# dt columns from the two f32r parts of h on the full array; one diagonal burst per scan group, two bursts per latent convolution tile

## The chip, the core and the metric

The kernel runs on one core of one Trainium2 chip. The metric is the device time of one execution in microseconds (us). Three runs of the kernel before the change took 1979.71, 1980.26 and 1985.91 us; the median is 1980.26 us. The profiled execution has a span of 1980.4 us from its first to its last instruction.

A core has these engines, named as the profile names them: PE (TensorE, matrix multiplication; its weight loads are listed apart as PEld and overlap the matmuls), DVE (VectorE), ACT (ScalarE), POOL (GpSimd) and SP (SyncE, from whose queue all DMAs of this kernel are issued). Each engine works through its own list of instructions in order, and waits where an operand is not there.

## The reference, cut to what matters

One layer of a diffusion backbone, for 256 context tokens and 2048 latent tokens, 1024 channels wide. All data are float32.

```python
h = rms_norm(x, g_pre) * (1 + scale) + shift
u = h @ w_in                       # 1024 x 5664
z, xbc, dt_raw, ga, gb, gsil = split(u)   # 1024, 1536, 32, 1024, 1024, 1024 columns
y_ssd, h_fin = ssd_branch(z, xbc, dt_raw, ...)     # two-way scan, 16 heads of 64, chunks of 128
y_conf = conformer_branch(ga, gb, ...) * silu(gsil)  # 31-tap convolution, layer norm
out = concat([y_ssd, y_conf]) @ w_out
return x + gate * rms_norm(out, g_post), h_fin
```

Three pieces of it are touched: `dt_raw`, the 32 columns of the input projection that give the step sizes of the scan; the part of the scan inside a chunk, `y_diag = (C B^T * decay) x`, one 128x128 matrix per head and chunk; and the 31-tap convolution of the latent tokens along the rows of a 32x64 grid.

## The kernel before, in words

**Stages.** The 2304 tokens are 18 chunks of 128, done in two halves of nine; a half is three blocks of 384 tokens. In each half `hprep` makes h for a block, transposed, channels on the partitions, in two f32r parts: `hh` (h rounded) and `hl` (the rest). Then tiles of 128 columns of `w_in` (also in two parts, `wh` and `wl`) are multiplied: `mm_cm` (L334) runs over eight slices k of the channels, with three matmuls of 128x384 each (L338 to L340), into the psum tiles `xp` (x, B, C), `gb`/`ga` (gate) and `sp` (z and gsil). `xbc_unit` and `conv5` follow each xp tile with a five-tap convolution on DVE. While the gb, ga and sp tiles run, the scan (`pass_a`, chunk by chunk) is woven in; in the first half with it the context convolution on DVE, in the second half the latent convolution (`lat_conv`, eight tiles of 128 channels). At the end comes the output projection (`op`, L1038).

**hprep (L237).** Per block: `pr` spreads the norm over the partitions (L271); for each of the eight slices k, DVE multiplies the slice `ht` by it (L285), ACT applies scale and shift (L288), and `split(k)` (L274) does the rest: the dt matmul on PE (L277), the cast to `hh` on DVE (L278), and the subtraction that gives `hl` on POOL, for every fourth slice on DVE (L279). The dt matmul is in plain f32 with 32 columns of weights; slice k goes to columns `32*(k%4)` of the array, so that `pd` holds four partial sums that L304 adds after a transposition.

**The scan (L606).** `pass_a(i)` is a generator of about ten steps per chunk, and the next chunk starts six steps after the one before. Each chunk has two groups g of eight heads, and each group two quarters hq of four heads with two directions. `load_lb` (L617) loads 256 KB of row data, spread to all partitions, into the tiles `lb` (four buffers per direction); `mask`, `decay` and `mix` make the 128x128 matrices of four heads out of them; `diag(g, hq)` (L671) then multiplies four of them on PE into `py`, each with 64 columns of weights (head j of a pair in columns 64j). `off` gives `po` (L684), `state` the three matmuls of `pst` (L690 to L692).

**The latent convolution (L559).** `expand(u)` (L574) copies taps into one of two buffers `kbuf`, eight small copies, four on DVE and four on ACT; then eight matmuls with 64 columns of weights go into `cp` (L592). There are four such rounds per tile, with a step between.

**What sets the order.** The generators are interleaved by hand (`interleave`, `merge`, `xbc_phase`), but the lists of the engines are set when the kernel is built: the program is scheduled with a timeline simulation (`schedule_with_timeline_sim=True`, L1182), which moves instructions by when it reckons that they can start. So the order of the source is a wish, and the lists are what stands. [...]

Of the kernel before, what the change touches and what calls it, by code (L numbers as in the profile page):

```python
# [8 lines left out]
F32 = mybir.dt.float32  # L9
F32R = mybir.dt.float32r  # L10
# [3 lines left out]
MUL, ADD, SUB, MAX, MIN = ALU.mult, ALU.add, ALU.subtract, ALU.max, ALU.min  # L14
# [31 lines left out]
def merge(a, na, b, nb):  # L46
    """The steps of two generators as one list, each spread evenly over it."""
    steps, x, y = [], 0, 0
    for _ in range(na + nb):
        if y * na >= x * nb and x < na or y >= nb:  # L50
            steps.append(a)
            x += 1
        else:
            steps.append(b)
            y += 1
    return steps
# [8 lines left out]
def backbone_kernel(ctx, tc, xa, xt_in, cols, rows, wconv, conf_b, gp_row, bg_row, state0, w_mod, w_dt, w_in, w_out,  # L65
# [8 lines left out]
    def bank(tag, name):  # L74
        return psp.tile([P, 512], F32, tag=tag, name=name, bufs=3 if tag == "mm" else 5)
# [75 lines left out]

    # ---------------------------------------------------------------- input projection, scan, convolutions
    ph_h = ExitStack()
# [26 lines left out]
    V.tensor_scalar(cfb2, cv[:, C_CONFB:C_CONFB + 8], 2.0, None, MUL)  # L180
    wdt = pa.tile([P, KT, 32], F32, name="wdt")
    DT = pa.tile([P, HTILES, 32], F32, name="DT")
# [4 lines left out]

    # ---- modulation
    sc = pa.tile([P, 2, 8], F32, name="sc")
# [12 lines left out]
    def modulation(h):  # L202
        """Shift and scale of one half of the channels, as columns."""
        mp = bank("mm", f"mp{h}")
        for k in range(KT):
            if h == 1 and k in (3, 4):
                wm = pa.tile([P, 2, 512], F32, tag=("xT", "el")[k - 3], name=f"wm{h}_{k}", bufs=1)
            elif h == 1 and k > 4:
                wm = cp.tile([P, 2, 512], F32, tag="x4", name=f"wm{h}_{k}", bufs=3)
            else:  # L210
                if k % 3 == 0:
                    b, tag = ((1, "a"), (1, "b"), (2, "a"), (2, "b"))[3 * h + k // 3]
                    wms, n = hps[b].tile([P, 3, 2, 512], F32, tag=tag, name=f"wm{h}_{k}"), 0
                wm = wms[:, n]
                n += 1
            DMA.dma_start(wm, w_mod[k * P:(k + 1) * P, 0:2 * D].rearrange("p (s c) -> p s c", s=2)[:, :, h * 512:(h + 1) * 512])
            for s in range(4):
                T.matmul(mp[32 * s:32 * s + 2, 0:256], sc[:, :, k], wm[:, s // 2, s % 2 * 256:s % 2 * 256 + 256],
                         start=(k == 0), stop=(k == KT - 1))
            yield  # L220
        mc = bank("ss", f"mc{h}")
        mr = slab(f"mr{h}")
        for s in range(4):
            (V.tensor_copy if s % 2 else S.copy)(mr[0:2, s * 256:(s + 1) * 256], mp[32 * s:32 * s + 2, 0:256])
            for q in range(2):
                c = 2 * s + q
                T.transpose(mc[:, 2 * c:2 * c + 2], mr[0:2, c * P:(c + 1) * P], ident[0:2, 0:2])
        m = mc[:, 0:16].rearrange("p (s k a) -> p s a k", s=2, k=4)
        ks = slice(4 * h, 4 * h + 4)
        bc4 = lambda c: cv[:, c + 4 * h:c + 4 * h + 4].unsqueeze(1).to_broadcast([P, 2, 4])  # L230
        V.scalar_tensor_tensor(S1[:, :, ks], m[:, 1], 1.0, bc4(C_BSC), ADD, ADD)
        V.tensor_tensor(S1[:, :, ks], S1[:, :, ks], bc4(C_GPRE), MUL)
        V.tensor_tensor(SH[:, :, ks], m[:, 0], bc4(C_BSH), ADD)
        yield

    # ---- normalised, modulated, transposed input of one block in two f32r parts; its dt columns
    def hprep(b, out):  # L237
# [34 lines left out]
        pd = bank("ss", f"pd{b}")  # L272

        def split(k):  # L274
            t = ts.pop(k)
            q = k % 4
            T.matmul(pd[q * 32:(q + 1) * 32, :BN], wdt[:, k, :], t, start=(k < 4), stop=(k >= 4))  # L277
            V.tensor_copy(hh[:, k, :], t)  # L278
            (V if k % 4 == 3 else G).tensor_tensor(hl[:, k, :], t, hh[:, k, :].bitcast(F32), SUB)  # L279

        for k in range(KT):
            if b > 0:
                load_t(k)
            t = ts[k]
            V.tensor_tensor(t, t, pr[:, :BN], MUL)  # L285
            parts = ((0, 256, 1), (256, BN, 0)) if b == 0 else ((0, BN, 0),)
            for c0, c1, a in parts:
                S.activation(t[:, c0:c1], t[:, c0:c1], AF.Identity, bias=SH[:, a, k:k + 1], scale=S1[:, a, k:k + 1])  # L288
            if k > 0 and not (b == 0 and k == 4):
                split(k - 1)  # L290
            if b == 0 and k == 3:
                split(k)
            yield
        split(KT - 1)
        yield
        d4 = ev(f"d4_{b}")
# [3 lines left out]
        for t in range(BLK):  # L300
            T.transpose(pt[:, t * P:(t + 1) * P], d4[:, t * P:(t + 1) * P], ident)
        yield
        t0 = (b % BLK) * BLK
        V.tensor_reduce(DT[:, t0:t0 + BLK, :], pt[:, :BN].rearrange("p (t q h) -> p t h q", t=BLK, q=4),  # L304
                        mybir.AxisListType.X, ADD)
        yield

    # ---- one tile of input-projection columns, split in two f32r parts
    def load_w(c0):
# [32 lines left out]

    # ---- dt: softplus, its logarithm, and the decays of every chunk
    def dt_post(half):
# [64 lines left out]

    # ---- x, B, C columns and their five-tap convolution along the tokens  # L410
    def xbc_unit(half, ct, hb, tails):
# [36 lines left out]
    def xbc_phase(half, first, hb, prep, tails, dtp):  # L448
        """The first tiles go block by block, while the next block is being prepared."""
        def tail_step():  # L450
# [57 lines left out]

    # ---- gate of the modulation times g_post, as two rows in DRAM
    def gate_rows():  # L510
# [23 lines left out]

    # ---- Conformer convolution of the context tokens, along the sequence
    def ctx_conv(j):
# [20 lines left out]

    # ---- Conformer convolution of the latent tokens, along the rows of the grid
    def lat_conv(j, lp, kbuf):  # L559
# [24 lines left out]
        yield  # L584
        expand(0)
        yield
        for u in range(4):
            kt = kbuf[u % 2]
            ps = bank("ss", f"cp{j}_{u}")
            for q in range(4):  # L590
                for h in range(2):
                    T.matmul(ps[h * 64:(h + 1) * 64, q * P:(q + 1) * P], x[:, h * 16 + u * 4 + q, :], kt[:, h * 4 + q, :],  # L592
                             start=True, stop=True)
            if u < 3:
                expand(u + 1)
            yield
            V.scalar_tensor_tensor(vt[:, ::-1, u * 16:(u + 1) * 16].rearrange("p r c -> p c r"),
                                   ps.rearrange("p (c r) -> p c r", r=32), 0.5,
                                   cbb[:, u * 16:(u + 1) * 16].unsqueeze(2).to_broadcast([P, 16, 32]), MUL, ADD)
# [4 lines left out]

    # ---- scan of one chunk: inside the chunk both ways, across chunks forward
    def pass_a(i):  # L606
# [63 lines left out]

        def diag(g, hq):  # L671
            if hq == 0:
                py[g] = bank("ss", f"py{i}{g}")
            for t in range(4):
                h = hq * 4 + t
                j, q = h % 2, h // 2
                T.matmul(py[g][j * HD:(j + 1) * HD, q * P:(q + 1) * P], xt[g][:, h * HD:(h + 1) * HD],
                         E[g, hq, 0][:, t, :], start=True, stop=True)

# [75 lines left out]
        yield  # L755
        diag(0, 0)
        off(0)
# [6 lines left out]
        yield  # L764
        diag(0, 1)
        state(0, 1)
# [4 lines left out]
        yield  # L771
        diag(1, 0)
        off(1)
        state(1, 0)
        weigh(1, 1)
        keep(0)
        close(0)
        mix(1, 1)
        yield
        diag(1, 1)  # L780
        state(1, 1)
# [10 lines left out]
    def scan(tiles):  # L792
        """Chunks in turn, each starting six steps after the one before it."""
        gens = [pass_a(i) for i in tiles]
        live, t = [], 0
        while gens or live:
            if gens and t % 6 == 0:
                live.append(gens.pop(0))
            for g in list(live):
                if next(g, 0) == 0:  # L800
                    live.remove(g)
            t += 1
            yield

    # ---- order of the work
    def interleave(blocks, side, n):
# [29 lines left out]
    run(modulation(0))  # L836
    DMA.dma_start(wdt.rearrange("p k n -> p (k n)"), w_dt)
    for _ in range(4):
# [57 lines left out]

    # ---------------------------------------------------------------- output projection
    ph_1 = ExitStack()
# [288 lines left out]
```

## Time and profile before

| | before |
|---|---|
| runs (us) | 1979.71, 1980.26, 1985.91 |
| median (us) | 1980.26 |
| span of the profiled execution (us) | 1980.4 |
| mean granted TensorE clock | 0.976 |
| busy, share of the span: PE, PEld | 96%, 85% |
| busy, share of the span: DVE, ACT, POOL | 64%, 44%, 42% |
| DMA: bytes moved, mean rate | 306.03 MB, 155 GB/s |

How to read the rows. A row of a timeline gives the start in us from the start of the span, the duration in us, the engine, the line, the operation, the tile written and those read, weights and result sizes, and how many records were merged into the row; what follows in brackets is the idle time of the engine before it and what ended it. Matmuls are pipelined and their ends are modelled, so the time that a matmul takes is read from one start to the next. A plain f32 matmul leaves two records (x2), an f32r matmul one; both are labelled f32. A row of windows gives, for a stretch of time, how long each engine was busy, the granted clock of PE, the DMA share and the rate.

### The profile page before, as it was taken

The page shows a single profiled execution, that of the slowest core. Times are in us where ns is not written, and L with a number is a line of the kernel's source. Part 1 is how long each engine was busy: PE and PEld are TensorE (multiplying, and loading weights), DVE is VectorE, ACT ScalarE, POOL GpSimd, SP SyncE. Part 2 cuts the span into 40 slices and gives each one's busy share as a digit, 9 for nine tenths or more (in the row PEclk, how much of TensorE's full clock was granted, in tenths as well). Part 3 has the DMA queues.
Part 4 walks back from the last instruction along what each step waited for, and adds up shares of the span by engine and source line. Part 5 has one row for each costly group of instructions (what it writes and reads, how often), then busy time and mean ns, then how long its engine had stood idle before and what let it go on. Part 6 is the DMA issues. An engine that isn't in the chain of part 4 may idle for free.

```text
span 1980.4 us, 29842 instructions
## 1 busy us (share of the span) xinstructions
PE 1892.3 (96%) x10796; PEld 1693.0 (85%) x10796; DVE 1273.9 (64%) x1776; ACT 869.1 (44%) x1973; POOL 830.0 (42%) x760
## 2 busy tenths in 40 slices
PE   7999999979998999998999999999999999999998
PEld 4699988979887897898999999989997878778776
DVE  2587768797765425878556665565438766776753
ACT  3447333443444523455356665664424333333332
POOL 2435243444443524544246455453226443454421
PEclk8999999989999999999999999999999999999999
DMA  8325453434344633233556667664947555555542
GB/s 294 118 93 158 138 145 123 121 107 133 118 144 135 207 134 106 96 112 112 153 148 190 189 194 212 177 192 148 282 155 198 160 163 155 176 169 156 161 131 78
DMA packets 285105, 306.03 MB, mean 155 GB/s; under 512 B 84630, under 2 KB 207382, under 8 KB 284956
## 3 DMA queue, kind: packets, MB, share of 16 engines
q1 hardware_dynamic: 284956, 304.12, 50.4%
q8 instruction: 85, 1.39, 0.3%
q14 instruction: 64, 0.52, 0.1%
HBM read 221.38 MB, written 82.67 MB: 154 GB/s over the span
## 4 chain that ended last, share of the span: by engine, by line
PE 54%; DVE 12%; DMA 6%; issue 4%; ACT 4%; POOL 2%; SPq 1%; DVEq 0%; POOLq 0%; ACTq 0%
PE op L1038 15%; PE sp L338 4%; PE sp L340 4%; PE sp L339 4%; DVE cg L546 4%; PE ga L338 2%; PE ga L340 2%; PE ga L339 2%; PE gb L338 2%; DVE cva L440 2%; PE gb L339 2%; PE gb L340 2%; DMA lb<-lt 2%; ACT lb L641 2%; PE cp L592 1%
## 5 line engine op out<-in xcount | busy, mean ns | idle before, releaser
L318 POOL TENSOR_TENSOR wl<-wr,wh 128x512 fp32r<-128x512 f32 x176 | 265.8, 1526 | 259.7 <-ACT wh L317 237.8
L338 PE MATMUL sp<-hh,wh 128*128 128x384 f32 x768 | 264.6, 344 | 11.9 <-DVE sth L506 11.8
L339 PE MATMUL sp<-hl,wh 128*128 128x384 f32 x768 | 260.9, 340 | 0.0
L340 PE MATMUL sp<-hh,wl 128*128 128x384 f32 x768 | 260.9, 340 | 0.0
L641 ACT ACTIVATE lb<-lb,WB 128x128 f32<-128x128 f32 x576 | 180.2, 390 | 93.9 <-POOL lb L633 89.3
L338 PE MATMUL xp<-hh,wh 128*128 128x384 f32 x576 | 199.6, 347 | 12.1 <-ACT raw L428 9.8
L340 PE MATMUL xp<-hh,wl 128*128 128x384 f32 x576 | 198.1, 344 | 0.3 <-POOL wl L318 0.3
L339 PE MATMUL xp<-hl,wh 128*128 128x384 f32 x576 | 198.4, 345 | 0.0
L633 POOL TENSOR_SCALAR_AFFINE_SELECT lb<-lb 128x512 f32<-128x512 f32 x144 | 118.2, 831 | 180.7 <-DMA lb<-lt 105.7
L440 DVE SCALAR_TENSOR_TENSOR cva<-raw,cwh,cva 128x1026 f32<-128x1026 f32 (+1 forms) x96 | 157.7, 1650 | 27.7 <-ACT cva L434 25.9
L317 ACT CAST wh<-wr 128x512 fp32r<-128x512 f32 x176 | 102.5, 616 | 136.3 <-DMA wr<-in_w_in 74.4
L338 PEld LDWEIGHTS sp<-hh,wh 128*128 128x128 f32 x768 | 145.7, 190 | 18.6 <-DVE sth L506 13.8
L546 DVE SCALAR_TENSOR_TENSOR cg<-cg,cv 128x256 f32<-128x256 f32 x240 | 156.6, 669 | 4.0
L339 PEld LDWEIGHTS sp<-hl,wh 128*128 128x128 f32 x768 | 145.9, 190 | 2.8 <-issue 1.6
L340 PEld LDWEIGHTS sp<-hh,wl 128*128 128x128 f32 x768 | 145.6, 190 | 2.1 <-issue 2.0
L1016 ACT ACTIVATE th<-ct,lnq 128x128 f32<-128x128 f32 x144 | 65.9, 457 | 184.9 <-PE ct L1012 84.2
L506 DVE SCALAR_TENSOR_TENSOR sth<-sth,sp 128x384 f32<-128x384 f32 x96 | 52.4, 550 | 136.1 <-ACT sth L505 130.6
L338 PE MATMUL ga<-hh,wh 128*128 128x384 f32 x384 | 132.8, 346 | 0.0
L340 PE MATMUL ga<-hh,wl 128*128 128x384 f32 x384 | 130.5, 340 | 2.2 <-POOL wl L318 2.2
L338 PE MATMUL gb<-hh,wh 128*128 128x384 f32 x384 | 131.9, 344 | 0.3 <-DVE gth L495 0.3
L339 PE MATMUL ga<-hl,wh 128*128 128x384 f32 x384 | 130.6, 340 | 0.0
L338 PEld LDWEIGHTS xp<-hh,wh 128*128 128x128 f32 x576 | 110.3, 192 | 23.5 <-ACT raw L428 11.3
(228 smaller groups left out, 4505.0 us busy)
## 6 DMA issues: line engine op xcount, KB each, us to landing
wr<-in_w_in SPq DMA_DIRECT2D x176, 256.0 KB, 3.2
lb<-lt SPq DMA_DIRECT2D x144, 256.0 KB, 3.9
ht<-in_xt SPq DMA_DIRECT2D x48, 192.0 KB, 3.3
xT<-xb SPq DMA_DIRECT2D x18, 512.0 KB, 5.4
gl<-gth SPq DMA_DIRECT2D x48, 192.0 KB, 2.5
yp<-yg SPq DMA_DIRECT2D x36, 256.0 KB, 3.9
st<-sb SPq DMA_DIRECT2D x36, 256.0 KB, 3.7
zs<-sth SPq DMA_DIRECT2D x48, 192.0 KB, 2.2
```

The costliest lines, as they stand in the source:

```text
L317: S.copy(wh[:, ks, :], wr)
L318: G.tensor_tensor(wl[:, ks, :], wr, wh[:, ks, :].bitcast(F32), SUB)
L338: T.matmul(ps[:, :BN], wh[:, k, :], hh[:, k, :], start=(k == 0), stop=False)
L339: T.matmul(ps[:, :BN], wh[:, k, :], hl[:, k, :], start=False, stop=False)
L340: T.matmul(ps[:, :BN], wl[:, k, :], hh[:, k, :], start=False, stop=(k == KT - 1))
L440: V.scalar_tensor_tensor(a[:, :n], raw[:, t:t + n], cwh[:, ct * 5 + t:ct * 5 + t + 1], a[:, :n], MUL, ADD)
L506: V.scalar_tensor_tensor(th, th, 1.0, ps[:, :BN], ADD, MUL)
L546: V.scalar_tensor_tensor(acc, g[:, t:t + 256], cv[:, w0 + t:w0 + t + 1], acc, MUL, ADD)
L633: G.affine_select(E[g, hq, d], E[g, hq, d], pattern=[[0, 4], [sg, P]], compare_op=ALU.is_ge, fill=NEG, base=0, channel_multiplier=-sg)
L641: S.activation(lb[:, h, :], lb[:, h, :], AF.Exp, bias=WB[:, i, c + h:c + h + 1])
L1016: S.activation(th[:, c, :], pc, AF.Tanh, bias=lnq[:, 1, k:k + 1], scale=lnq[:, 0, k:k + 1])
L1038: T.matmul(pso[n], lhs[:, k % 8, :], w[:, n * 512:(n + 1) * 512], start=(k == 0 and m == 0), stop=(k == 15 and m == 2))
```

## The change

Three things are rewritten, and the lists of all engines are scheduled anew.

**dt columns.** `split` no longer issues the dt matmul. A new `dt_cols(k)` issues two f32r matmuls per slice, with `hh` and with `hl`, over the full 128 columns of the array. The weights `wdt` are an f32r tile in which slice k has 64 columns: 32 of the rounded weights, 32 of the rest; the matmul takes 128 columns from there on, so the upper 64 rows of `pd` hold products that nobody reads. It is issued three steps later than the slice is prepared, and the last three after a further step. L304 now adds two partial sums, not four. The weights are loaded to `wdr`, and split once by two small DVE operations.

**Diagonal matmuls.** `diag(g)` issues the eight matmuls of a group in one go, at the step where the second quarter was before. `mix(1, 1)` moves ahead of `keep(0)` and `close(0)`.

**Latent convolution.** `expand(0)` and `expand(1)` go first, then the matmuls of rounds 0 and 1 together, `expand(2)` and `expand(3)`, a step, then rounds 2 and 3 together. A tile has five steps where it had seven.

Beside that the scratch memory for dynamic DMAs is set to 1024 bytes, which makes room in SBUF, and comments are gone.

```diff
-    wdt = pa.tile([P, KT, 32], F32, name="wdt")
+    wdr = pa.tile([P, KT, 32], F32, name="wdr")
+    wdt = pa.tile([P, KT * 64 + 64], F32R, name="wdt")
+    G.memset(wdt[:, KT * 64:].bitcast(F32), 0.0)
...
+        def dt_cols(k):
+
+            w = wdt[:, k * 64:k * 64 + P]
+            T.matmul(pd[:, :BN], w, hh[:, k, :], start=(k == 0), stop=False)
+            T.matmul(pd[:, :BN], w, hl[:, k, :], start=False, stop=(k == KT - 1))
+
         def split(k):
             t = ts.pop(k)
-            q = k % 4
-            T.matmul(pd[q * 32:(q + 1) * 32, :BN], wdt[:, k, :], t, start=(k < 4), stop=(k >= 4))
             V.tensor_copy(hh[:, k, :], t)
...
+            if k > 2:
+                dt_cols(k - 3)
             yield
         split(KT - 1)
+        yield
+        for k in range(KT - 3, KT):
+            dt_cols(k)
         yield
...
-        V.tensor_reduce(DT[:, t0:t0 + BLK, :], pt[:, :BN].rearrange("p (t q h) -> p t h q", t=BLK, q=4),
+        V.tensor_reduce(DT[:, t0:t0 + BLK, :], pt[:, :BN].rearrange("p (t q h) -> p t h q", t=BLK, q=4)[:, :, :, 0:2],
...
         expand(0)
-        yield
+        expand(1)
+        yield
+        ps2 = {}
         for u in range(4):
-            kt = kbuf[u % 2]
-            ps = bank("ss", f"cp{j}_{u}")
-            for q in range(4):
-                for h in range(2):
-                    T.matmul(ps[h * 64:(h + 1) * 64, q * P:(q + 1) * P], x[:, h * 16 + u * 4 + q, :], kt[:, h * 4 + q, :],
-                             start=True, stop=True)
-            if u < 3:
-                expand(u + 1)
-            yield
+            if u % 2 == 0:
+                for v in (u, u + 1):
+                    ps2[v] = bank("ss", f"cp{j}_{v}")
+                    for q in range(4):
+                        for h in range(2):
+                            T.matmul(ps2[v][h * 64:(h + 1) * 64, q * P:(q + 1) * P], x[:, h * 16 + v * 4 + q, :],
+                                     kbuf[v % 2][:, h * 4 + q, :], start=True, stop=True)
+                if u == 0:
+                    expand(2)
+                    expand(3)
+                yield
+            ps = ps2.pop(u)
...
-        def diag(g, hq):
-            if hq == 0:
-                py[g] = bank("ss", f"py{i}{g}")
-            for t in range(4):
-                h = hq * 4 + t
+        def diag(g):
+            py[g] = bank("ss", f"py{i}{g}")
+            for h in range(8):
                 j, q = h % 2, h // 2
                 T.matmul(py[g][j * HD:(j + 1) * HD, q * P:(q + 1) * P], xt[g][:, h * HD:(h + 1) * HD],
-                         E[g, hq, 0][:, t, :], start=True, stop=True)
+                         E[g, h // 4, 0][:, h % 4, :], start=True, stop=True)
...
-        diag(0, 0)
         off(0)
...
-        diag(0, 1)
+        diag(0)
...
-        diag(1, 0)
         off(1)
         state(1, 0)
         weigh(1, 1)
+        mix(1, 1)
         keep(0)
         close(0)
-        mix(1, 1)
-        yield
-        diag(1, 1)
+        yield
+        diag(1)
...
-    DMA.dma_start(wdt.rearrange("p k n -> p (k n)"), w_dt)
+    DMA.dma_start(wdr.rearrange("p k n -> p (k n)"), w_dt)
+    wd4 = wdt[:, 0:KT * 64].rearrange("p (k q n) -> p k q n", q=2, n=32)
+    V.tensor_copy(wd4[:, :, 0, :], wdr)
+    V.tensor_tensor(wd4[:, :, 1, :], wdr, wd4[:, :, 0, :].bitcast(F32), SUB)
```

Three places in the list of PE show how the instructions stand. The first is the start of block 1 in the first half; `xp_2_0` is the projection of the third column tile for block 0, `xp_0_1` and its fellows are those for block 1, `pd` is the dt tile of block 1. Before, from the last of the `pr` matmuls of block 1 on:

```order
L271 MATMUL pr_582<-ident,xr_577 128x128
L340 MATMUL xp_2_0_552<-hh_179,wl_85_392 128x384
L338 MATMUL xp_2_0_552<-hh_179,wh_85_393 128x384
L339 MATMUL xp_2_0_552<-hl_180,wh_85_393 128x384
...
L277 MATMUL pd_586<-ht_0_587,wdt 32x384
L338 MATMUL xp_2_0_552<-hh_179,wh_85_393 128x384
L339 MATMUL xp_2_0_552<-hl_180,wh_85_393 128x384
L277 MATMUL pd_586<-ht_1_597,wdt 32x384
L277 MATMUL pd_586<-ht_2_607,wdt 32x384
```

And now:

```order
L273 MATMUL pr_594<-ident,xr_589 128x128
L279 MATMUL pd_598<-hh_568,wdt 128x384
L349 MATMUL xp_0_1_690<-hh_568,wh_87_375 128x384
L349 MATMUL xp_1_1_769<-hh_568,wh_86_385 128x384
L349 MATMUL xp_2_1_830<-hh_568,wh_85_395 128x384
L280 MATMUL pd_598<-hl_569,wdt 128x384
L279 MATMUL pd_598<-hh_568,wdt 128x384
```

Before, 22 projection matmuls of block 0 stood between `pr` and the first that needs `hh` of block 1; now there is none, since those of `xp_2_0` moved up into block 0. At `pr` of block 2, 21 projection matmuls stand there now.

The second place is the start of block 4 in the second half, where `xp_2_0` is again a projection for the block before. Before:

```order
L277 MATMUL pd_7144<-ht_4_7202,wdt 32x384
L339 MATMUL xp_2_0_7267<-hl_6891,wh_41_7095 128x384
L277 MATMUL pd_7144<-ht_5_7215,wdt 32x384
L340 MATMUL xp_2_0_7267<-hh_6890,wl_41_7094 128x384
L277 MATMUL pd_7144<-ht_6_7225,wdt 32x384
L338 MATMUL xp_2_0_7267<-hh_6890,wh_41_7095 128x384
```

And now:

```order
L279 MATMUL pd_7180<-hh_7150,wdt 128x384
L349 MATMUL xp_2_0_7305<-hh_6918,wh_41_7131 128x384
L350 MATMUL xp_2_0_7305<-hl_6919,wh_41_7131 128x384
L351 MATMUL xp_2_0_7305<-hh_6918,wl_41_7130 128x384
...
L280 MATMUL pd_7180<-hl_7151,wdt 128x384
L279 MATMUL pd_7180<-hh_7150,wdt 128x384
```

The matmuls with 32 columns are gone; two of full width per slice, one with `hh` and one with `hl`, took their place, and the first needs `hh` where only `ht` was needed before. Between `pr` of this block and the first `pd` now stand 46 projection matmuls of the block before.

The third place is a group of the scan in the second half. Before, a burst of four `py` matmuls stood ahead of `po`, and the second, later, ahead of `pst`:

```order
L340 MATMUL ga_1_1_8938<-hh_7114,wl_28_8555 128x384
L677 MATMUL py_8945<-lb_8682,xt_8815 64x128 x4
L684 MATMUL po_8950<-bc_8679,Sf_173 128x128 x4
L690 MATMUL pst_8955<-xwh_8870,bth_8809 128x512
L691 MATMUL pst_8955<-xwl_8871,bth_8809 128x512
```

Now `po` follows a projection directly, and the eight `py` matmuls stand together where the second four stood:

```order
L351 MATMUL gb_1_2_9068<-hh_7351,wl_29_8597 128x384
L691 MATMUL py_9081<-lb_8734,xt_8867 64x128 x4
L691 MATMUL py_9081<-lb_8830,xt_8867 64x128 x4
L704 MATMUL pst_9090<-xwh_9007,bth_8861 128x512
L705 MATMUL pst_9090<-xwl_9008,bth_8861 128x512
```

Over the whole list the bursts of `py` go from 72 to 36, those of `cp` from 31 to 17 (the four rounds of the last tile stood in two bursts already), and the 44 bursts with `pd` are gone.

More of the change, by code (lines that the diff above doesn't have):

```diff
@@ L1177 @@
     arrays = {f"in_{k}": np.ascontiguousarray(v) for k, v in arrays.items()}
-    nc = _bacc.Bacc("TRN2", target_bir_lowering=False, num_devices=1)
+    nc = _bacc.Bacc("TRN2", target_bir_lowering=False, num_devices=1, dynamic_dma_scratch_size=1024)
     args = [nc.dram_tensor(k, v.shape, mybir.dt.from_np(v.dtype), kind="ExternalInput").ap() for k, v in arrays.items()]
```

## The prediction

> **What bounds the kernel now.** I read the engines' shares, then the stretches with the granted clock, then the timeline of PE around the instructions that change.
>
> ```profile
> PE 1892.3 (96%) x10796; PEld 1693.0 (85%) x10796; DVE 1273.9 (64%) x1776; ACT 869.1 (44%) x1973; POOL 830.0 (42%) x760
> 60.00:100.00 40.00, 39.52 (x191) 27.58 (x190) 26.13 (x42) 15.10 (x29) 15.62 (x15) 1.00 0.30 100
> 260.00:500.00 240.00, 222.86 (x1310) 208.55 (x1309) 191.82 (x300) 97.94 (x254) 98.32 (x99) 0.96 0.41 120
> 745.00:810.00 65.00, 65.00 (x303) 45.09 (x303) 38.05 (x63) 26.11 (x51) 29.53 (x30) 1.00 0.35 108
> 1000.00:1250.00 250.00, 250.00 (x1725) 227.61 (x1723) 150.57 (x239) 161.26 (x424) 133.23 (x127) 1.00 0.64 187
> ```
>
> The reader sees that PE is the bound. In 745 to 810, where half of the dt matmuls stand, and in 1000 to 1250, with the second scan and the latent convolution, it never idles: a microsecond saved on PE there is one saved at the end, unless another engine becomes late. Only the first scan (260 to 500) leaves PE 17 us idle at 0.96 of the clock, beside a DVE busy for 80%.
>
> **The price of a dt matmul.** Durations overlap, so I take starts.
>
> ```profile
> L277 PE MATMUL pd<-ht,wdt 128*32 128x384 f32 x96 | 39.9, 527 | 4.6 <-ACT ht L288 4.6
> 752.96 0.34 PE L339 MATMUL sp<-hl,wh 128*128 128x384 f32 x1
> 753.23 0.83 PE L277 MATMUL pd<-ht,wdt 128*32 128x384 f32 x2
> 753.99 0.44 PE L340 MATMUL sp<-hh,wl 128*128 128x384 f32 x1
> 754.36 0.83 PE L277 MATMUL pd<-ht,wdt 128*32 128x384 f32 x2
> 755.12 0.45 PE L338 MATMUL sp<-hh,wh 128*128 128x384 f32 x1
> 755.40 0.33 PE L339 MATMUL sp<-hl,wh 128*128 128x384 f32 x1
> 755.58 0.34 PE L340 MATMUL sp<-hh,wl 128*128 128x384 f32 x1
> 69.51 0.84 PE L277 MATMUL pd<-ht,wdt 128*32 128x384 f32 x4
> ```
>
> A projection matmul follows the next by 0.175 us (755.40 to 755.58). From 752.96 to 755.40 pass 2.44 us with three of them (0.525) and two dt matmuls: 0.96 each. A new one is a pair of the projection's own form (f32r, 128x384, full width), 0.35. There are 48 (96 records, two for each). Two neighbours run together and cost as one (the x4 row): in the second half 24 stand in 23 bursts, in blocks 1 and 2 there are 16 in 13.
>
> Second half: 23 x 0.96 less 24 x 0.35 is **13.7 us**, all in a stretch where PE never idles. What could hold it back is the preparation of the next block, since the first `pd` now waits for `hh`, not `ht`. The first half shows how long that takes:
>
> ```profile
> 60.43 0.83 PE L271 MATMUL pr<-ident,xr 128*128 128x128 f32 x6
> 61.30 3.81 DVE L285 TENSOR_TENSOR ht<-ht,pr 128x384 f32<-128x384 f32 x8
> 65.09 3.42 DVE L278 CAST hh<-ht 128x384 fp32r<-128x384 f32 x5
> 66.17 4.47 POOL L279 TENSOR_TENSOR hl<-ht,hh 128x384 fp32r<-128x384 f32 x4
> 78.62 0.83 PE L271 MATMUL pr<-ident,xr 128*128 128x128 f32 x6
> ```
>
> DVE does its eight products first, so the first `hh` is there 5.4 us after `pr` (65.09 and one cast of 0.7), the first `hl` some 1.5 us later (66.17 and a quarter of 4.47), and then one per 1.1. In the second half 46 projection matmuls, 8.0 us, stand between `pr` and the first `pd`: that covers it, and I cost the wait at nothing. Without that cover it is the first half's case.
>
> There, blocks 1 and 2 save 13 x 0.96 less 16 x 0.35, 6.9 us, and block 0 at most 8 x 0.61, 4.9. But the list has nothing left between `pr` of block 1 and its `hh`: 5.4 less 0.6 for `pr` itself, 4.8 us idle. At block 2 the 21 matmuls (3.7 us) leave 1.1. And the clock falls:
>
> ```profile
> 337.56 0.79 PE L691 MATMUL pst<-xwl,bth 128*128 128x512 f32 x1 [3.47 <-DVE xwl L668]
> 340.46 0.34 PE L338 MATMUL ga<-hh,wh 128*128 128x384 f32 x1
> ```
>
> After 3.47 us of idling matmuls take twice as long for 2.9 us, a loss of 1.4. So 11.8 less 4.8, 1.1 and 1.4 leaves 4.5; since PE also waited in block 0 for `ht` (the 4.6 of the group row), part of block 0's saving only lengthens a wait: I take **3 us**, bounds 0 and 11.
>
> **The price of a burst.** A burst of 64-column matmuls has edges:
>
> ```profile
> 1000.82 0.34 PE L340 MATMUL ga<-hh,wl 128*128 128x384 f32 x1
> 1001.09 1.09 PE L592 MATMUL cp<-kbuf,cx 128*64 128x128 f32 x16
> 1002.12 0.44 PE L338 MATMUL ga<-hh,wh 128*128 128x384 f32 x1
> 1002.40 0.33 PE L339 MATMUL ga<-hl,wh 128*128 128x384 f32 x1
> 1402.35 1.97 PE L592 MATMUL cp<-kbuf,cx 128*64 128x128 f32 x32
> 1404.25 0.44 PE L340 MATMUL sp<-hh,wl 128*128 128x384 f32 x1
> 1004.65 0.34 PE L340 MATMUL ga<-hh,wl 128*128 128x384 f32 x1
> 1004.92 0.66 PE L677 MATMUL py<-lb,xt 128*64 128x128 f32 x8
> 1005.51 1.16 PE L684 MATMUL po<-bc,Sf 128*128 128x128 f32 x8
> 1006.42 0.47 PE L690 MATMUL pst<-xwh,bth 128*128 128x512 f32 x1
> 310.02 0.34 PE L340 MATMUL gb<-hh,wl 128*128 128x384 f32 x1
> 310.19 0.60 PE L653 MATMUL px<-ident,xT 128*128 128x128 f32 x4
> 310.55 0.42 PE L338 MATMUL gb<-hh,wh 128*128 128x384 f32 x1
> 310.81 0.34 PE L339 MATMUL gb<-hl,wh 128*128 128x384 f32 x1
> ```
>
> Start to next start, 16 records take 1.03 and 32 take 1.90: 0.054 each, so 16 are 0.87. The way in costs 0.27 less 0.175, the way out 0.16 (1.03 less 0.87) and another 0.105 on the matmul behind (0.28 less 0.175): **0.36 per burst** that goes. The `px` rows, f32 but full width, show no cost on the way in (310.02 to 310.19) and 0.085 on the way out: the last part belongs to the f32 form.
>
> Scan: 36 bursts go, the instructions stay. 34 of them stood ahead of `po`, which is f32 and leaves to f32r later anyhow; there only 0.095 and 0.155 (0.59 less eight records) go, 0.25. With two of the full price: **9.2 us**; bounds 8.5 and 13. [...]
>
> Latent convolution: 31 bursts become 17, 14 x 0.36 is **5.0 us**. What is late next are the copies:
>
> ```profile
> L581 ACT COPY kbuf<-kd x128: 404/424/487, 972.3 to 1407.3; 32x128 f32<-32x128 f32 x128
> SPq L621 <- PE py L677: 32.2, 14, 4.6
> ```
>
> Two expansions are eight copies on ACT, 3.4 us, now all between two bursts of a tile; the new list has at least 29 other matmuls there, over 5 us with `po` and `pst` among them. I allow 1 us over eight tiles. Of the scan's saving, 16 of 36 groups lie in the first scan, where PE waits for DVE: half of their 4.0 is taken off, 2. The smaller sum in L304 and the two new DVE operations weigh nothing: DVE has 36% free.
>
> Sum: 13.7 + 3 + 9.2 + 5.0 - 1 - 2 = 27.9. The profiled span of 1980.4 is 0.1 over the median of the runs shown, so the forecast is **1952 us**.
>
> **Rivals.** *Preparation bounds both halves* (chance 0.18). If the 46 matmuls in front of `pd` are not enough because DVE takes L506 or the copies first, PE stalls twice more as in block 1, 6.2 us with the clock each; the first half brings nothing. For it: one chain of 5.4 us; against: 8.0 us of cover. Then 13.7 - 12.4 + 9.2 + 5.0 - 3 is 12.5: 1968 us.
>
> *All of it arrives* (0.08): the waits of block 0 shrink with it and the full edge price goes in the scan: 13.7 + 11 + 13 + 5, 1938 us.
>
> *Nothing to see* (0.08): as the first rival, and the scan's waits grow by what it saves: 1977 us.
>
> *Slower, through `lb`* (0.08). The buffer of a chunk's first quarter is free one step later, just when the next chunk wants to load it. SP's queue then stands at that load, as it did 14 times for 2.3 us (the SPq row), and weight loads are queued behind; POOL's masks and the `py` burst come late. At 17 chunks that is 39 us if each such hold reaches PE whole: 1980.4 - 27.9 + 39, 1992 us. It decides from 1.6 us per chunk on. Against it: the loaded tile is also needed one step later, so the chain has as many steps as before, and in 1000 to 1250 PE never idled, whatever SP held.
>
> **How the numbers follow.** The forecast has 0.58. Runs of this kernel tell 0.3% from nothing, 6 us. Forecast, first rival and full sum are faster: 0.84; the same 0.08; slower 0.08. The range reaches from the full sum, 1937, to the first rival with 2 us more, 1970; outside lie the last two cases and the edges.
>
> **What would show it.** The `pd` group with 96 f32r matmuls and no start-to-start over 0.2 us around it; `py` in bursts of x16 with 1.0 to 1.1 us to the next start; PE busy without a gap between `pr` and `pd` in blocks 3 to 5, and one of 4 to 5 us before `pd` of block 1; the stretch from 745 on 13 to 14 us shorter. It is wrong if the idle time of PE grows by over 10 us anywhere, above all in waits for `kbuf`, `lb` or `hl`.

## The result

| | before | after |
|---|---|---|
| median of the runs (us) | 1979.99 | 1997.88 |
| lowest to highest | 1977.78 to 1985.91 | 1995.80 to 2001.62 |
| span of the profiled execution (us) | 1980.4 | 1999.8 |
| mean granted TensorE clock | 0.976 | 0.968 |

The ratio after to before is 1.0084, with a 95% interval of 1.006 to 1.0109: about 17 us slower, where 28 us faster was predicted. The profiled execution is the slowest of the four after (2001.62 us).

### The profile page after: what moved, and what is told of

The parts are those of the page before. It is cut to its first block, busy times and chain, and to the rows that moved or that the text cites. A ratio compares the mean times of both kernels' runs of the same rounds, so it can differ in the third digit from the quotient of the medians.

```text
span 1999.8 us, 29798 instructions
## 1 busy us (share of the span) xinstructions
PE 1870.9 (94%) x10796; PEld 1723.7 (86%) x10796; DVE 1269.9 (64%) x1778; ACT 869.1 (43%) x1973; POOL 825.0 (41%) x761
## 5 line engine op out<-in xcount | busy, mean ns | idle before, releaser
L349 PEld LDWEIGHTS xp<-hh,wh 128*128 128x128 f32 x576 | 111.9, 195 | 24.8 <-ACT raw L439 15.6
```

The source lines that it names most:

```text
L349: T.matmul(ps[:, :BN], wh[:, k, :], hh[:, k, :], start=(k == 0), stop=False)
```

## The profile after

The page of the changed kernel, shares of the engines, and below it the same four stretches that were shown of before (busy time of PE, PEld, DVE, ACT, POOL, then clock, DMA share and rate):

```profile
PE 1870.9 (94%) x10796; PEld 1723.7 (86%) x10796; DVE 1269.9 (64%) x1778; ACT 869.1 (43%) x1973; POOL 825.0 (41%) x761
...
60.00:100.00 40.00, 33.78 (x181) 32.65 (x180) 24.41 (x39) 14.67 (x30) 14.37 (x14) 0.91 0.26 84
260.00:500.00 240.00, 222.82 (x1307) 211.06 (x1306) 192.66 (x300) 96.13 (x247) 105.61 (x99) 0.95 0.40 119
745.00:810.00 65.00, 64.82 (x381) 64.42 (x380) 38.36 (x63) 31.85 (x66) 31.46 (x33) 1.00 0.37 114
1000.00:1250.00 250.00, 237.72 (x1702) 220.24 (x1701) 151.37 (x254) 161.14 (x429) 119.98 (x117) 0.99 0.69 193
```

PE is busy for 21.4 us less than before (1870.9 against 1892.3): the work did get shorter. But span less busy time went from 88.1 to 128.9 us: 40.8 us of new idling ate it nearly twice over. In 1000 to 1250, where PE never idled before, 12.3 us are idle now. DVE and ACT do about what they did (61% and 64% busy), and POOL does less, 119.98 us for 133.23.

The timeline of PE shows that the prices were right. First the start of block 1, then a grouped burst of the scan:

```profile
69.70 0.66 PE L279 MATMUL pd<-hh,wdt 128*128 128x384 f32 x1 [4.26 <-DVE hh L284]
...
1028.02 1.09 PE L691 MATMUL py<-lb,xt 128*64 128x128 f32 x16
1029.05 0.50 PE L704 MATMUL pst<-xwh,bth 128*128 128x512 f32 x1
```

A gap of 4.26 us stands before `pd` of block 1 (4.8 predicted), and a burst of 16 records takes 1.03 us to the next start. The longest waits of PE between 1000 and 1410 us, where before there were 1.6 us in all (engine, line, what it waited for, us in total, times, longest). `sth` and `gth` are the operations of DVE that read a projection out of psum and so free its bank (the kernel takes three banks for the projections, tag mm); `xwh` and `xwl` are the two parts of what `pst` multiplies:

```profile
PE sp L349 <- DVE sth L517: 7.6, 2, 4.0
PE pst L705 <- DVE xwl L684: 6.1, 5, 2.0
PE gb L349 <- DVE gth L506: 3.2, 2, 2.1
PE pst L705 <- POOL xwl L684: 2.2, 2, 1.9
```

Where the time goes is seen best if the start of the same projection or output matmul, by its count within its tile name, is taken from the timelines of PE of two kernels. The table gives that difference to the kernel before, in us, from one profiled execution each, at six places named by their time before; a step between two columns is what the stretch between them cost or brought.

| | 740 (end of first half) | 816 (dt, second half) | 994 | 1286 (second scan, latent) | 1491 (output starts) | 1973 |
|---|---|---|---|---|---|---|
| the change | +1.9 | -12.2 | -10.2 | +17.7 | +12.8 | +19.0 |
| dt alone | +2.5 | -11.9 | -9.0 | -8.6 | -6.2 | -8.8 |
| grouped bursts alone | +2.4 | +2.6 | 0.0 | +4.6 | +6.4 | +4.0 |
| latent part alone | -0.4 | -0.3 | -1.3 | +23.7 | +13.6 | +12.7 |
| six lb buffers | -24.4 | -24.4 | -22.4 | -22.7 | -25.5 | -21.8 |
| six, grouped bursts | -19.4 | -19.3 | -19.3 | -23.4 | -27.2 | -28.9 |
| six, dt and grouped | -18.0 | -28.1 | -30.5 | -34.0 | -38.2 | -38.8 |
| six, whole change | -18.0 | -30.2 | -28.7 | -8.6 | -15.5 | -15.6 |

The first row says: dt in the second half brought 14.1 us, the second scan with the latent convolution lost 28, of which 5 came back when the latent tiles were done early. The other rows are the experiments.

## Experiments: the parts one by one

Each kernel is the one before with only the named part of the change's diff. What follows "Measured" is the ratio of its time to that of the kernel before, run beside it, with the 95% interval.

**dt alone.**

> Only the dt part on the kernel before (f32r pairs, full array, smaller scratch memory). All theories agree here on the second half: the stretch from 745 to 810 us shortens by 13 to 14 us; the first half brings about 0, since in the profile of the whole change the gain there was used up by the wait before pd of block 1. So 1980 less 12 to 16, about 1966 us. If it is within 5 us of the kernel before, the dt part too is spent later (a better-fed PE meets the same DVE and POOL).

Measured: 0.9953 (0.994 to 0.9967), 9 us faster. The second half brings 14.4 us between 740 and 816 (table); ahead of it 2.5 are lost, and the stages behind it take 3 back. That is less than the 12 to 16 expected.

**Grouped bursts alone.**

> Only the grouped diagonal bursts on the kernel before. Theory A (the lb tiles come free and are loaded a step later, the masks on POOL wait for them, and xwl and xw stand behind these in the queues): slower, +8 to +25 us (1988 to 2005), and the waits of POOL's mask for the lb loads grow. Theory B (the pairs of expansions of the latent convolution fill DVE and ACT in front of xwl and sth): faster by 7 to 9 us, about 1972. Theory C (neither part alone, only the lists of the engines as scheduled anew): anything within 6 us.

Measured: 1.0047 (1.0031 to 1.0064), 9 us slower. The profiled execution (1986 us) is the fastest of its eight, so the table shows only 4 of the 9.

**Latent convolution alone.**

> Only the latent convolution in two bursts per tile. Theory A: faster by 3 to 5 us, about 1976. Theory B: slower by 10 to 25 us, 1990 to 2005, with PE waiting for xwl and sth between 1000 and 1400 us. Theory C: within 6 us.

Measured: 1.0081 (1.0067 to 1.0096), 16 us slower, all of it lost between 994 and 1286.

**dt and grouped bursts.**

> The dt part and the grouped diagonal bursts, the latent convolution as before. Theory A: as the whole change, 1990 to 2005. Theory B: 1980 less 15 less 8, about 1957. Theory C: the sum of the two parts measured alone, within 5 us, if the lists are no matter; off by more than that if they are.

Measured: 1.0001 (0.9987 to 1.0015). The three parts add up: -0.47%, +0.47% and +0.81% make the +0.81% that the whole change shows (0.84), and -0.47% and +0.47% the 0.01% of this run. So the times that theory A gave for the grouping and theory B for the latent part came, and theory C, that neither part alone matters but only the newly scheduled lists, did not: two parts lose, each by itself. Why they do is not shown by these four runs.

## Experiments: the latent part

Its tile takes five steps where it took seven, and `merge` still deals 48 slots to it: the eight tiles have 40 steps, so all of them fall into five sixths of a stretch that held 48/7, not quite seven, before. Rate and form changed together. The next two runs part them.

```diff
         expand(0)
+        yield
         expand(1)
         yield
...
-                    expand(3)
                 yield
             ps = ps2.pop(u)
+            if u == 0:
+                yield
+                expand(3)
```

> The latent convolution in two bursts per tile, but with seven steps per tile as before, so that its eight tiles are spread over the same stretch as before. The latent part alone cost 16 us. Theory B1 (rate: five steps for seven at the same interleaving pack the copies, evacuations and loads of a tile into 29 us where they had 40): the loss goes, within 5 us of the kernel before or up to 5 us faster. Theory B2 (two expansions at once stand in front of xwl, sth and gth on DVE and ACT): the loss stays, +10 to +20 us.

Measured: 1.0011 (0.9998 to 1.0025). And the kernel before, with its four bursts, in five steps:

```diff
             if u < 3:
                 expand(u + 1)
-            yield
+            if u % 2 == 0:
+                yield
```

> The kernel before with its four bursts per tile, but five steps per tile instead of seven: the rate alone. Theory B1: slower by 10 to 20 us, with PE idle between 1000 and 1300 us as in the latent part alone. Theory B2: within 5 us of the kernel before.

Measured: 1.0125 (1.0107 to 1.0144), 25 us slower, more than the 10 to 20 expected. The rate is what costs. At the same rate the pairs even help, by 0.44%; at the old rate they do not bring the 0.25% that they were to bring.

Why more work per time hurts while no engine is full was asked with six `lb` buffers (next section), so that late loads of the scan weigh less. The whole change then still loses to the same kernel without the latent part:

> The whole change with six lb buffers per direction. With them alone the kernel took 1961 us, with the grouped bursts 1954. Theory A (what the change lost, the grouping's 9 and the denser latent convolution's 16 us, it lost through late lb loads): 1954 less 9 to 14 for dt and 0 to 5 for the pairs, 1935 to 1946 us. Rival (the denser latent convolution costs by its own copies and loads on DVE, ACT and SP, whatever the lb buffers): 10 to 16 us more, 1950 to 1962 us.

Measured: 0.9923 (0.9897 to 0.9949), 1968 us. That is 23 us above the same kernel without the latent part (next section), so more `lb` buffers do not take this loss away, and theory A fails here. The loss is larger than the rival's 10 to 16 us.

> The whole change with six lb buffers and seven steps per latent tile. Theory A: as the whole change with six buffers, 1935 to 1946 us. The rival: faster than that one by 10 us or more, and within 5 us of the run without the latent part.

Measured: 0.9831 (0.9801 to 0.986), 1950 us. Seven steps give 18 us back here too. Holding of SP's queue by the tile's own loads was tried with four `lb` buffers, with `bufs=2` for `kd` and `cx`:

> The latent part alone (five steps per tile), four lb buffers, but two buffers each for the taps kd and the tile cx, so that SP's queue isn't held by their loads (scratch memory smaller, for room). It cost 16 us with one buffer. If the lb loads are late because they queue behind held kd and cx loads: under 6 us slower than the kernel before. If they are late because their own buffers come free late (DVE and PE that use them are later): still 10 to 18 us slower.

Measured: 1.0085 (1.0052 to 1.0118): no better than 1.0081 with one buffer. (This run has the smaller scratch memory too, and the latent part alone has not; it makes no difference that shows.) Then work was left out of the whole change with six buffers, one kind at a time. First DVE's copies after the first tile, then (with 1 in place of 0) ACT's, then the loads after the first tile:

```diff
                     eng = S.copy if c4 % 2 else V.tensor_copy
+                    if j > 0 and c4 % 2 == 0:
+                        continue
```

> The whole change with six lb buffers (1968 us), without DVE's expansion copies after the first latent tile (the output of the latent convolution is not the reference's). With seven steps per tile the same kernel took 1950 us, the floor for these runs. If the loss lies in DVE's queue (copies and evacuations in front of xwl, sth and gth, stretched while POOL works): 1948 to 1956. If it lies elsewhere: 1963 to 1969.

Measured: 0.9834 (0.9807 to 0.986), as with seven steps: the loss is gone. No run leaves these copies out at seven steps, so this says that the loss does not come without DVE's copies, and not that they alone make it. Late `lb` loads are not the loss: the waits of POOL's masks for them between 1000 and 1410 us are 40.7 us here, 47.2 with the copies, and 24.7 without the latent part.

> The same without ACT's expansion copies after the first tile, DVE's kept (part of the computation left out again). If the loss lies in ACT's queue (copies of 0.42 us, 3.4 us per pair of expansions, in front of xwh, wh and the exponentials): 1948 to 1956. If elsewhere: 1963 to 1969. If both queues carry a part, both runs land between 1955 and 1963.

Measured: 0.9894 (0.987 to 0.9919), about a third of it back; the interval overlaps that of the whole change with six buffers.

> The same with all copies, but the loads of kd, cx and cbb only for the first tile (the later tiles compute on the first one's data). If the loss lies in SP's queue or the DMA engines: 1948 to 1956. If it lies in the copies: 1963 to 1969.

Measured: 0.9895 (0.9857 to 0.9932), overlapping too: a part from the loads is possible and not shown. Next all work is kept, and the 40 steps are spread over the whole stretch:

```diff
-merge(sc_, 60, extra, 8 * 6)
+merge(sc_, 60, extra, 8 * 5)
```

> The whole change with six lb buffers, all work kept, its 40 latent steps spread evenly over the stretch (66 units of eight matmul triples' steps per tile, where five steps packed at the old interleaving take 55 and seven took 77). If the rate sets the loss, it goes in part or whole: 1950 to 1960. If it is the form (pairs within one step), it stays: 1963 to 1969.

Measured: 0.9891 (0.9859 to 0.9923), again about a third, with overlapping intervals. By the count in the expectation the rate is only partly back, 66 units a tile for 77. Last, all copies go to ACT:

```diff
-                    eng = S.copy if c4 % 2 else V.tensor_copy
+                    eng = S.copy
```

> The whole change with six lb buffers, all expansion copies on ACT, none on DVE; all work kept. If the copies cost through DVE (in front of gth, sth and xwl, and stretched while POOL works): 1948 to 1958 us, though ACT then has 6.8 us of copies per pair of expansions. If any queue that holds them loses as much: 1963 us or more.

Measured: 0.991 (0.9879 to 0.9941). Moving the copies leaves most of the loss where leaving them out takes all of it. It does not tell DVE's queue from the copies as such: PE now waits for ACT's copies themselves, as rows below show. Back at four buffers, the change without DVE's copies:

> The whole change as it stands (four lb buffers, 1998 us), without DVE's expansion copies after the first tile (the output of the latent convolution is not the reference's). If they cause the latent part's loss here too, 13 to 22 us less: 1976 to 1985, the kernel with dt and the grouped bursts alone (1982) or a little less. If with four buffers it is the late lb loads that the denser tiles make: 1990 to 1998.

Measured: 1.0008 (0.9986 to 1.0031): without DVE's copies the change as it stands loses nothing to its other two parts (1.0001). So taking DVE's copies away takes away the latent part's 16 us with four buffers as well.

How copies of a quarter of a microsecond can do that is seen at one place of the whole change with six buffers. The timeline of DVE, POOL and PE, with PE's weight loads and unbracketed matmuls left out:

```profile
1131.65 1.09 DVE L613 SCALAR_TENSOR_TENSOR cvv<-cp,cbb 128x512 f32<-128x512 f32 x1
1132.30 2.53 POOL L329 TENSOR_TENSOR wl<-wr,wh 128x512 fp32r<-128x512 f32 x2 [2.52 <-ACT wh L328]
1132.59 3.39 DVE L592 COPY kbuf<-kd 32x128 f32<-32x128 f32 x3
1134.79 1.07 POOL L710 TENSOR_TENSOR Sf<-Sf,eTf 128x512 f32<-128x512 f32 x1
1136.01 0.69 DVE L682 TENSOR_TENSOR xw<-xt,WS 128x512 f32<-128x512 f32 x1
1136.62 0.55 DVE L506 SCALAR_TENSOR_TENSOR gth<-gth,ga 128x384 f32<-128x384 f32 x1
...
1137.22 0.69 PE L349 MATMUL gb<-hh,wh 128*128 128x384 f32 x1 [4.08 <-DVE gth L506]
...
1294.23 0.95 DVE L592 COPY kbuf<-kd 32x128 f32<-32x128 f32 x4
```

Three copies that need 0.24 us each (the last row has four in 0.95) take 3.39 us while POOL works beside them. Behind them in DVE's list stand `xw` and then `gth`, which has to free a psum bank of the projections; PE waits 4.08 us for it. Without DVE's copies PE idles far less; windows from 970 to 1300 us, the whole change with six buffers first, then the run without DVE's copies:

```profile
970.00:1300.00 330.00, 315.83 (x2267) 294.63 (x2265) 206.87 (x340) 218.28 (x577) 163.81 (x159) 0.98 0.70 196
```

```profile
970.00:1300.00 330.00, 327.58 (x2382) 308.05 (x2381) 177.79 (x244) 222.49 (x585) 170.28 (x165) 0.99 0.72 204
```

DVE's work falls by 29 us, PE's idle time by 11.8. Some of that work is the copies themselves, so this is not their delay alone. With all copies on ACT, PE waits for the copies, here for the two bursts of a tile:

```profile
1254.68 1.40 PE L606 MATMUL cp<-kbuf,cx 128*64 128x128 f32 x16 [2.61 <-ACT kbuf L592]
1257.64 2.28 PE L606 MATMUL cp<-kbuf,cx 128*64 128x128 f32 x16 [1.56 <-ACT kbuf L592]
```

## Experiments: the grouped bursts

Theory A said that the tile of a chunk's first quarter comes free one step later, so that the next chunk's load, the mask on POOL, and `xwl` and `xw` behind it come late. More buffers take that reason away and leave the grouping: `bufs=4` becomes `bufs=6` for `lb` (and for `ht`, which shares them), in the smaller scratch memory of the change.

> The grouped diagonal bursts with six lb buffers per direction in place of four (scratch memory smaller, for room). The diagonal part alone cost 9 us. Theory A (the lb tiles come free a step later, the loads and so the masks are late): the loss goes and the edges of the bursts come through, 1980 less 2 to 9, and POOL's masks wait less than 40 us for lb loads between 1000 and 1410 us (38 before, 53 with the diagonal part alone). Rival (lists and the in-order queues on DVE and ACT, whatever the buffers): still +5 to +12 us.

Measured: 0.9857 (0.9843 to 0.9871), 28 us faster.

> The kernel before with six lb buffers per direction, nothing else (scratch memory smaller): the control for the run with the grouped bursts. Theory A: within 5 us of the kernel before, since PE hardly waited on the scan in its second half; faster by up to 6 us if the waits of the first scan (17 us idle between 260 and 500 us) hang on the same loads. If it gains as much as the grouped bursts do with six buffers, the buffers are worth something by themselves and say nothing on the grouping.

Measured: 0.989 (0.9872 to 0.9907), 22 us faster than before. So the control gained far more than expected, and the buffers are worth most of it. The two runs together speak on the grouping: it costs 9 us with four buffers, and brings 0.33%, 6.5 us, with six. So its loss hangs on the buffers. The lists are scheduled anew for each kernel, and a share can lie there: PE's list differs at 232 of 10796 places between the grouped bursts with four and with six, and at 227 between the kernel before and its control.

The waits of POOL's masks for the `lb` loads between 1000 and 1410 us follow, of the kernel before, with the grouped bursts, of the control, and with the grouped bursts and six buffers:

```profile
POOL lb L633 <- DMA lb<-lt: 38.4, 17, 6.9
```

```profile
POOL lb L633 <- DMA lb<-lt: 52.7, 18, 6.9
```

```profile
POOL lb L633 <- DMA lb<-lt: 18.5, 16, 3.3
```

```profile
POOL lb L633 <- DMA lb<-lt: 28.9, 14, 6.2
```

The grouping adds 14.3 us to them with four buffers and still 10.4 with six, where the kernel is faster all the same. So a growth of these waits does not by itself cost time; with four buffers, where they are longer, the grouping loses.

The loads themselves are no faster with six buffers (4.3 us to landing, as a median, against 3.9 before): they start earlier. In the second scan 13.0 us pass from the issue of a load to the start of a mask, in order of their counts and as a median, with six buffers alone; before it was 5.3. The six buffers alone gain all they gain in the first half (table, 740), as the windows of the first scan show (PE was busy 222.86 us in the first stretch before, and 228.07 in the second):

```profile
260.00:500.00 240.00, 227.33 (x1353) 212.17 (x1352) 194.44 (x300) 93.54 (x238) 100.19 (x98) 0.98 0.43 124
500.00:745.00 245.00, 238.62 (x1392) 221.85 (x1391) 133.78 (x208) 102.08 (x238) 105.15 (x96) 0.98 0.48 149
```

PE's idle time falls from 17.1 to 12.7 us in the first stretch and from 16.9 to 6.4 in the second: what the prediction read there as a busy DVE hung in part on the `lb` loads.

**The version that beats both kernels** has dt, the grouped bursts and six buffers, and the latent convolution as before:

> As the run above without the latent part (four bursts, seven steps). Both theories: 1954 less 9 to 14, 1940 to 1946 us. Theory A: the run above is the same or faster by up to 5 us; the rival: the run above is slower by 10 us or more.

Measured: 0.9814 (0.9786 to 0.9842), 1945.6 us. Its windows over the second scan:

```profile
1000.00:1410.00 410.00, 408.90 (x2825) 383.82 (x2824) 246.11 (x383) 242.15 (x606) 200.98 (x183) 1.00 0.68 201
```

PE is busy for 99.7% of the stretch in which it idled 24 us in the change.

## Why the prediction was wrong

**The bound.** The reading was right: before the change PE never idled in 1000 to 1250. The step from it, "a microsecond saved on PE there is one saved at the end, unless another engine becomes late", hung on its second half, which was looked at for each edit's own neighbours only. DVE was taken to have room ("DVE has 36% free"). It has room on average, but at the place of 1132 us above it had none when a projection's psum bank waited for it.

**dt, second half: right.** 13.7 us predicted; 14.1 within the change and 14.4 alone. The 46 matmuls ahead of `pd` covered the preparation, as said: PE is busy for 64.82 of the 65 us.

**dt, first half: the term was mis-sized.** 3 us predicted within 0 to 11, about 0 measured: at the matmul that started at 229 us before, the change stood at +1.9, dt alone at +0.9. Kernels without the dt part stand between -2.5 and +1.9 there, so one profile tells this to about 2 us. The waits for the preparation came as worked out: 4.26 us before `pd` of block 1 for 4.8, and 0.67 in block 2 for 1.1. The slow clock behind the first of them was priced too low. The granted clock was 0.50 from 68.7 to 75.5 us, and 18 matmuls from 69.70 on take 5.87 us, 0.33 each, where 0.175 each would be 3.15: 2.7 us for the 1.4 predicted. So the 6.9 us of blocks 1 and 2 are used up. The saving of block 0, at most 4.9, went into longer waits, as the prediction feared for a part of it: between 25 and 60 us PE idles 12.3 us, where before it idled 7.2, and 6.21 of them are one wait for the weights `wh` from ACT.

Of the 16.7 us for dt as a whole 9 stayed; part of the rest went into new waits such as this one of the change, where PE had not waited before (1.35 us at the same matmul with dt alone):

```profile
843.87 0.69 PE L349 MATMUL xp<-hh,wh 128*128 128x384 f32 x1 [2.40 <-ACT raw L439]
```

**Grouped bursts: price right, cover wrong.** A burst of 16 records takes 1.03 us to the next start, and `po` eight records in 0.81 where it took 0.91, as predicted. With six buffers the grouping brings 4.8 us between 994 and 1491 (7.9 with it, 3.1 without), and 20 of 36 groups at 0.25 are 5.0. With four it loses 9. No run shows the 13 us for the scan, 36 bursts at 0.36 each, that is its upper bound and part of the 1938 us of the full sum; the gain of 4.8 with six buffers and the loss of 9 with four were measured in its place. The step that failed is the argument against the rival through `lb`, "the loaded tile is also needed one step later, so the chain has as many steps as before". The tile is needed later, but by the source the next chunk's first load goes into the buffer that this chunk's burst frees, and that burst moved into the very step of the load. With six buffers the load goes into a buffer that is free some steps earlier, and the loss turns into a gain. The rival named the right buffers with a chance of 0.08 and a price of 39 us; measured, it is about 16 (9 lost and 6.5 not gained). By itself it would have left the change faster. Its path is not what the trace shows: the holds of SP at `lb` loads behind `py` fell with the grouping alone, from 32.2 us (14 times) to 13.5 (7), and those behind DVE's sum of two `lb` tiles (L645) grew from 81.1 to 108.1, little of it in the second half (43.4 to 46.9 between 816 and 1500 us). On which hold the loss depends stays open.

**Latent convolution: the step that turned the sign.** 5.0 less 1 predicted, 16 us lost. The prediction counted bursts on PE and asked whether two expansions fit between two bursts of a tile. It did not count steps: five for seven, at the same slots, raise the rate of copies, reads out of psum and loads by 40%. The rate alone, with the bursts as before, costs 25 us, and the pairs at the old rate cost nothing that shows (1.0011). The prediction also gave the copies' price as ACT's, "3.4 us, now all between two bursts of a tile", and left out DVE's share. Without that share the loss is gone; without ACT's about a third of it is. No rival held this.

**The sum.** The parts added up, so nothing is left for an interplay: -9, +9 and +16 in place of -16.7, -7.2 and -4. Of the signs given for "wrong", "PE idle time grows by over 10 us anywhere, above all in waits for `kbuf`, `lb` or `hl`", the size was met, but `kbuf` shows as 1.6 us in PE's own waits: PE waits above all for `sth`, `gth` and `xwl`. That the copies stand in front of those in DVE's list was seen at one place (`gth`, 1132 us) and not counted over the whole stretch.

**Open.** In the first scan the grouping loses time around 640 to 690 us with four buffers and with six, so that at 740 the grouped bursts stand 5 us behind the control (-19.4 for -24.4). PE's waits for `sth` between 620 and 700 us are 9.7 us where they were 5.8, and with six buffers 6.8 where the control has none; why is not settled. Nor is why pairs at the old rate bring nothing (1.0011; with six buffers 0.9831 against 0.9814 without them). How the latent loss splits between copies in the way and copies stretched is open too. DVE's 128 copies took 50.4 us in all before and 52.4 in the change, so the change hardly added to the stretching. With six buffers they took 51.5 us without the latent part and 59.6 with it.

## What to carry to other kernels

In a hand-made interleaving the number of a generator's steps sets its rate. Whoever merges two steps into one makes that generator run faster against all that it is woven into, so its slots have to be set anew, and the work per time on the other engines compared with what it was. When an edit holds a buffer longer, look at which load goes into that buffer next and at which step it is issued; here two buffers more turned a loss of 9 us by the edit into a gain of 6.5. Time saved on a PE that never idles arrives at the end only as long as the engines that free its psum banks keep up: here, between 1000 and 1410 us PE waited 12.1 us for `sth` and `gth` in the change, and not at all before.

## What the runs showed of the hardware

Some of DVE's operations took longer while POOL worked: copies from SBUF to SBUF, up to 1.38 us for a median of 0.28, and products of two SBUF tiles, up to 1.79 us for 0.69; `cvv` and `sth`, which read PSUM, did not. Here are the expansion copies in the whole change with six buffers, grouped by engine (count, then shortest, median and longest in ns, first and last start in us):

```profile
L592 DVE COPY kbuf<-kd x128: 242/280/1377, 945.3 to 1301.8; 32x128 f32<-32x128 f32 x128
L592 ACT COPY kbuf<-kd x128: 402/424/458, 945.7 to 1297.8; 32x128 f32<-32x128 f32 x128
```

ACT's all take about the same; DVE's longest takes five times its median. Of DVE's 128 copies 75 ran with no instruction of POOL beside them, and 11 started before the one of POOL that overlapped them: none of these took over 0.29 us. The other 42 started while an instruction of POOL ran; they took 0.86 us in the mean, and 40 of them ended 0.11 to 0.16 us after that instruction did. So nearly every copy that came second here ended just after POOL's instruction, and none that came first was slowed. With four buffers it looks the same: before the change 30 of the 128 copies came second and took 0.78 us in the mean, in the change 31 and 0.84, and 29 of them in each ended 0.11 to 0.17 us after POOL's instruction. Why a copy is held up so is not shown by the traces. Products of two SBUF tiles (`lb` with `cb`) take 0.69 us alone and 1.24 beside POOL, longest 1.79, though part of a longer one is more time in which to be overlapped. Those that read PSUM do not change: `cvv` 1.07 and 1.08, `sth` 0.55 and 0.55.
